# Late modulation and scaled output weights computed by halves of 512 columns, in one or two tiles of h at a time

## The chip, the cores and the metric

The kernel runs on one core of one Trainium2 chip. The metric is the device time of one execution in microseconds, the median of several. Five queues issue instructions in their own order and wait for each other through semaphores: PE (matmuls), DVE (vector), ACT (scalar), POOL (GpSimd) and SP, which here only issues DMA transfers. The program is one straight run without loops on the chip. A list scheduler of the framework fixes the order on each queue when the program is built; the kernel's Python code gives the dependencies and, by the order in which it records work, the priorities.

## The reference

One decoder layer over 2048 tokens of width 1024, in float32. A conditioning vector gives six vectors of 1024 (shift, scale and gate for each of the two sub-layers); two kinds of attention (8 heads each) run side by side; then one output projection, and a gated MLP with a convolution.

```python
mod = jax.nn.silu(c) @ w_ada[l] + b_ada[l]
shift_a, scale_a, gate_a, shift_m, scale_m, gate_m = [
    m[:, None, :] for m in jnp.split(mod, N_MOD, axis=-1)]
h = rms_norm(x, g_attn[l]) * (1.0 + scale_a) + shift_a
proj = h @ w_in[l]
q_f, k_f, v_f, q_s, k_s, v_s, f_logit = jnp.split(proj, offsets, axis=-1)
...
mix = jnp.concatenate([head_rms_norm(o_fox, g_out_fox[l]),
                       head_rms_norm(o_sb, g_out_sb[l])], axis=-1)
x = x + gate_a * (mix @ w_out[l])
h = rms_norm(x, g_mlp[l]) * (1.0 + scale_m) + shift_m
u = causal_depthwise_conv(h @ w_up[l], conv_w[l], conv_b[l])
u_gate, u_val = jnp.split(u, 2, axis=-1)
x = x + gate_m * ((jax.nn.silu(u_gate) * u_val) @ w_down[l])
return rms_norm(x, g_final)
```

The change touches four of the six vectors, those that are needed only after attention: `gate_a` (part 2 of `w_ada`), `shift_m` (3), `scale_m` (4) and `gate_m` (5); and the product of `w_out` with `gate_a` and the heads' gains.

## The kernel before

**Precision.** Each operand of a matmul is split into a high and a low part (`split`, lines 44 to 46: ACT copies and rounds, then DVE or POOL subtracts); a product is three matmuls.

**First half: units of attention.** There are 32 units (line 807): kind `sb` then `fox`, four pairs of heads p each, four blocks tb of 512 tokens each. Unit i's attention (`attend`) is the main stream. Beside it runs `ahead`, the projections of later units. For a unit (kind, p, tb) the projection `proj` (lines 463 to 473) loads the eight split tiles of the normalized input from DRAM, `hp<-hs` (line 468, 512 KB each, named `hs{tb}_{kt}`), and multiplies each at once: L342 for q and k, L413 for v. q, k and v go through DRAM (`qk_fox`, `vs_fox`) and are loaded again per unit as Q, K, V (lines 362 to 364). For each `fox` pair the running sums of the forget gate are loaded as `Fb` (line 653), 4 times 512 KB.

**The tiles of h.** `h_tile()` (line 155) takes one of ten tiles of 128 x 2 x 512 (512 KB) from the pool `sl`, all under one tag. The projections' `hs` loads and the late modulation share these ten; `wide()` (line 158) is the same tile seen as 128 x 1024.

**Late modulation** (`late_mod`, line 756, with `fold_out`, line 743) is a filler. From unit 12 on, `interleave` (line 109) records `PER` of its steps per unit (line 862: `LATE, PER = 12, 3`). For each of four parts it adds up, over eight blocks kt of 128 rows, `w_ada` times the column of `silu(c)`: a load (L776), then ACT scales it (L782) and POOL adds it to `wsum` (L783; L780 for the first). `wsum` holds one tile of h, each load takes another. For the two gates a third tile, `gt`, takes the broadcast `b_ada`; PE sums `wsum` over the partitions with a matmul of ones (L790), DVE adds (L791). For `gate_a`, `fold_out` then loads the eight row blocks of `w_out` (L746, a tile each), multiplies on DVE (L749), splits each half into another tile of h and stores it to `wos` (L753); `gt` stays held for the whole of it. `gate_m` is stored (L796). For shift and scale, eight matmuls of one column (L800) and an add (L802) make the columns `mod_m`.

**Behind it.** At unit 30 the code drains what is left of `ahead` and of `late_mod`, closes the pool `sl` and opens `big` in its place; the output weights are loaded from `wos` (`first_mix`, line 939) and the output projection begins (L912), first beside the last unit's attention. From there to the end the order is mostly fixed by hand (`fixed`, line 206): output projections, then the MLP's matmuls (L1315, L1614).

SP has one queue: a DMA that waits at its head holds back all behind it. Its DMAs also take turns on eight completion semaphores, so a new DMA waits until the one eight places ahead of it has landed.

## Time and profile before

| what | us |
|---|---|
| median of 3 runs | 2948.92 (2948.36 to 2949.31) |
| span of the profiled execution, first to last instruction | 2941.4 |
| its own full time | not on the page; the median less the span is 7.5 |
| PE busy | 2867.8 (97%) |
| DVE, ACT, POOL busy | 2179.5, 1686.0, 901.1 |
| mean granted TensorE clock | 0.993 |

A row of a profile gives engine, line of the kernel, operation, tiles written and read, shape, count and duration. A row of waits says who waited for whom, the sum in us, how often, and the longest. In a timeline a row begins with start and duration, and a bracket at its end gives the idle time before it and what ended it. In a table of windows the columns are the window, its length, busy time of PE, PE's weight loads, DVE, ACT and POOL with their instructions, the granted clock of PE as a share of full speed, the busy share of the DMA engines and the GB/s that they moved.

### The profile page before, as it was taken

Reading aid. Unit: us, or ns where it says so; the run is one execution under the profiler, and the core shown is the slowest. Engines: PE = TensorE matmul, PEld = TensorE weight load, DVE = VectorE, ACT = ScalarE, POOL = GpSimd, SP = SyncE. Lnnn points to the kernel's source line nnn. Section 1 sums busy time; section 2 is a strip of 40 time slices with the busy share of each in tenths; the row PEclk is TensorE's granted clock in tenths of the full one; section 3 lists DMA queues with packets and bytes.
Section 4 is the critical chain, followed back from the end, with each engine's and each line's share of the span. In section 5 each row is a group of like instructions: output and inputs, shape, how many; then the busy total and the mean of one; then the engine's idle time right before and its main releaser. Section 6 shows DMA issues by size and latency. Waiting matters only on the chain.

```text
span 2941.4 us, 45922 instructions
## 1 busy us (share of the span) xinstructions
PE 2867.8 (97%) x15772; PEld 2459.7 (84%) x15772; DVE 2179.5 (74%) x3464; ACT 1686.0 (57%) x3187; POOL 901.1 (31%) x967
## 2 busy tenths in 40 slices
PE   8999999999999999999999999999999999999998
PEld 7888888888988988888888788888788888888887
DVE  5787778877886656658843788888998888575476
ACT  5776767677776656658744554444444445433342
POOL 0431322243032423231213344444254543142200
PEclk8999999999999999999999999999999999999999
DMA  9749756867469794794537775554754444975644
GB/s 293 255 139 321 236 188 207 301 211 229 162 212 356 269 277 139 232 323 140 182 120 233 245 232 128 130 136 129 236 132 125 130 130 132 309 257 185 216 158 151
DMA packets 348346, 601.89 MB, mean 205 GB/s; under 512 B 34672, under 2 KB 178800, under 8 KB 348112
## 3 DMA queue, kind: packets, MB, share of 16 engines
q1 hardware_dynamic: 324208, 558.06, 57.7%
q0 software_dynamic: 10880, 20.97, 4.3%
q10 hardware_dynamic: 13024, 19.93, 1.9%
q8 instruction: 124, 2.03, 0.3%
q14 instruction: 110, 0.90, 0.1%
HBM read 420.77 MB, written 177.02 MB: 203 GB/s over the span
## 4 chain that ended last, share of the span: by engine, by line
PE 46%; DMA 3%; DVE 2%; SPq 1%; ACT 1%; issue 1%; POOL 0%; DVEq 0%; ACTq 0%; POOLq 0%
PE ps_o L1315 19%; PE ps_t L1315 7%; PE ps_o L1614 6%; PE ps_t L1614 3%; PE ps_bc L1614 3%; PE ps_o L912 1%; PE ps_pv L615 1%; DMA r<-rstd 1%; PE ps_bc L912 1%; PE ps_pt L606 1%; PE ps_o L1609 1%; DMA wo<-wos 1%; DMA hm<-hf_m 1%; SPq L895 1%; DVE op L46 1%
## 5 line engine op out<-in xcount | busy, mean ns | idle before, releaser
L1315 PE MATMUL ps_o<-op,wu 128*128 128x512 f32 x2592 | 608.0, 389 | 2.0 <-DVE snap L1366 1.5
L1315 PEld LDWEIGHTS ps_o<-op,wu 128*128 128x128 f32 x2592 | 486.2, 188 | 103.9 <-DVE snap L1366 1.9
L611 DVE TENSOR_TENSOR at<-ps_pt,at 128x512 fp32r<-128x512 f32 (+1 forms) x576 | 366.1, 652 | 100.2 <-ACT at L610 97.3
L636 DVE TENSOR_TENSOR_SCAN a<-r,a 128x512 f32<-128x512 f32 (+2 forms) x320 | 368.3, 1167 | 77.8 <-ACT a L631 39.9
L342 PE MATMUL ps_pj<-hp,w_qk 128*128 128x512 f32 x1512 | 411.2, 403 | 14.5 <-DMA hp<-hs 12.9
L610 ACT ACTIVATE at<-ps_pt 128x512 fp32r<-128x512 f32 (+1 forms) x576 | 318.5, 576 | 139.1 <-PE ps_pt L606 123.1
L615 PE MATMUL ps_pv<-at,V 128*128 128x256 f32 x2216 | 386.8, 292 | 9.3 <-DVE at L611 4.2
L615 PEld LDWEIGHTS ps_pv<-at,V 128*128 128x128 f32 x2216 | 320.9, 190 | 39.8 <-DVE at L611 11.4
L342 PEld LDWEIGHTS ps_pj<-hp,w_qk 128*128 128x128 f32 x1512 | 275.4, 190 | 71.0 <-DMA hp<-hs 16.2
L45 ACT ACTIVATE wu<-wuraw 128x512 fp32r<-128x512 f32 x204 | 128.9, 632 | 248.5 <-PE ps_o L1315 190.1
L596 PE MATMUL ps_qk<-K,Q 128*128 128x512 f32 (+2 forms) x640 | 265.7, 416 | 5.6 <-ACT a L631 3.3
L413 PE MATMUL ps_pj<-w_v,hp 128*128 128x256 f32 (+1 forms) x1536 | 236.6, 288 | 2.1 <-DVE hp L422 1.6
L597 PE MATMUL ps_qk<-K,Q 128*128 128x512 f32 (+2 forms) x640 | 235.7, 369 | 0.0
L1315 PE MATMUL ps_t<-op,wu 128*128 128x512 f32 x888 | 220.8, 390 | 1.0 <-DVE op L46 1.0
L413 PEld LDWEIGHTS ps_pj<-w_v,hp 128*128 128x128 f32 x1536 | 209.0, 189 | 10.9 <-DVE q L373 1.5
L630 ACT ACTIVATE r<-ps_qk 128x512 f32<-128x512 f32 (+2 forms) x320 | 173.1, 541 | 58.2 <-PE ps_qk L597 55.5
L46 DVE TENSOR_TENSOR wu<-wuraw,wu 128x512 fp32r<-128x512 f32 x204 | 189.6, 930 | 18.1 <-ACT wu L45 16.7
L1315 PEld LDWEIGHTS ps_t<-op,wu 128*128 128x128 f32 x888 | 166.4, 188 | 36.5 <-DVE op L46 1.8
L606 PE MATMUL ps_pt<-edge,a 128*128 128x128 f32 x1088 | 185.1, 274 | 8.4 <-DVE a L636 7.8
L1614 PE MATMUL ps_o<-op 128*128 128x512 f32 x840 | 191.5, 389 | 0.0
L1614 PEld LDWEIGHTS ps_o<-op 128*128 128x128 f32 x840 | 157.7, 188 | 32.7
L679 ACT ACTIVATE p<-p,mn 128x128 f32<-128x128 f32 (+15 forms) x128 | 153.9, 1203 | 53.3 <-DVE mn L675 52.2
(342 smaller groups left out, 5237.6 us busy)
## 6 DMA issues: line engine op xcount, KB each, us to landing
hp<-hs SPq DMA_DIRECT2D x224, 512.0 KB
wuraw<-in_w_up_dram SPq DMA_DIRECT2D x80, 512.0 KB
ra<-g SPq DMA_DIRECT2D x136, 256.0 KB
rb<-in_w_down_dram SPq DMA_DIRECT2D x108, 256.0 KB
g<-u SPq DMA_DIRECT2D x80, 256.0 KB
hs<-hp SPq DMA_DIRECT2D x32, 512.0 KB
hp<-in_w_ada_dram SPq DMA_DIRECT2D x32, 512.0 KB
qk_fox<-q SPq DMA_DIRECT2D x32, 512.0 KB
```

What stands on the lines that cost most here:

```text
L46: (lo_engine or nc.gpsimd).tensor_sub(lo, src, f(hi))
L342: nc.tensor.matmul(acc, w[kt][:, a, n], h[:, bb], start=kt == 0 and i == 0, stop=kt == KT - 1 and i == 2)
L413: nc.tensor.matmul(av[:, t * width:(t + 1) * width], hts[kt][:, a, tok], w[1][kt][:, bb, 0:width], start=kt == 0 and m == 0, stop=kt == KT ...
L596: nc.tensor.matmul(b[:, :cw], Q[:, hl, 0, qcols], K[:, hl, :cw], start=True, stop=False)
L597: marks.append(nc.tensor.matmul(b[:, :cw], Q[:, hl, 1, qcols], K[:, hl, :cw], start=False, stop=True).ins)
L606: nc.tensor.transpose(b[:, i * P:(i + 1) * P], blk(kts[kk], qi), ident)
L610: copies = [nc.scalar.activation(at[:, 0, lo:], b[:, lo:], AF.Copy).ins, nc.vector.tensor_sub(at[:, 1, lo:], b[:, lo:], f(at[:, 0, lo:])).ins]
L611: nc.vector.tensor_sub(at[:, 1, lo:], b[:, lo:], f(at[:, 0, lo:])).ins]
L615: m = nc.tensor.matmul(o[:, 0:2 * P], V[kt // 4][:, kt % 4, hl, :], rhs, start=first and kk == 0 and w == 0, stop=last and kk == 1 and w == 1)
L636: nc.vector.tensor_tensor_scan(rev, r[:, 0:need][:, ::-1], rev, 0.0 if right[qi] is None else right[qi][:, 0:1], ALU.mult, ALU.add)
L1315: nc.tensor.matmul(b, w[:, p, j], o[:, q], start=first and i == 0, stop=last and i == 2, skip_group_check=True)
L1614: nc.tensor.matmul(b, a[:, p, t * P:(t + 1) * P], w[:, q], start=first and i == 0, stop=last and i == 2, skip_group_check=True)
```

## The change

All four parts are now computed in two halves of 512 columns. One tile of h per half holds both the sum (`wsum`, its first 512 columns) and the load (`w`, the other 512), so that a load waits until POOL has added the one before it. The broadcast `b_ada` goes into `w`, the gate is made there, and `fold_out` (now called once per half, with the gate in `w`) loads its blocks of `w_out` into the place of `wsum` and takes one other tile of h for each split. The number of `yield`s goes from 56 to 90, and `PER` from 3 to 5.

```diff
-    def fold_out(gt):
+    def fold_out(n, gt, raw):
+        sl = slice(n * TB, (n + 1) * TB)
         for kt in range(KT):
-            raw = wide()
-            nc.sync.dma_start(raw, w_out[kt * P:(kt + 1) * P, :])
-            for n in range(2):
-                sl = slice(n * TB, (n + 1) * TB)
-                nc.vector.scalar_tensor_tensor(raw[:, sl], raw[:, sl], cols[:, R_GF + kt:R_GF + kt + 1], gt[:, sl],
-                                               ALU.mult, ALU.mult)
-                w = h_tile()
-                split(w[:, 0], w[:, 1], raw[:, n * TB:(n + 1) * TB])
-                nc.sync.dma_start(wos[kt][:, :, n * TB:(n + 1) * TB], f(w))
-                yield
+            nc.sync.dma_start(raw, w_out[kt * P:(kt + 1) * P, sl])
+            nc.vector.scalar_tensor_tensor(raw, raw, cols[:, R_GF + kt:R_GF + kt + 1], gt, ALU.mult, ALU.mult)
+            w = h_tile()
+            split(w[:, 0], w[:, 1], raw)
+            nc.sync.dma_start(wos[kt][:, :, sl], f(w))
+            yield
...
         for part, gate in late:
-            wsum = wide()
-            for kt in range(KT):
-                w = wide()
-                nc.sync.dma_start(w, w_ada[kt * P:(kt + 1) * P, part * D:(part + 1) * D])
-                for n in range(0, D, 512):
-                    sl = slice(n, n + 512)
+            for n in range(2):
+                two_ = f(h_tile())
+                wsum, w = two_[:, 0], two_[:, 1]
+                sl = slice(part * D + n * TB, part * D + (n + 1) * TB)
+                for kt in range(KT):
+                    nc.sync.dma_start(w, w_ada[kt * P:(kt + 1) * P, sl])
                     if kt == 0:
-                        nc.gpsimd.tensor_scalar_mul(wsum[:, sl], w[:, sl], cs[:, 0:1])
+                        nc.gpsimd.tensor_scalar_mul(wsum, w, cs[:, 0:1])
                     else:
-                        nc.scalar.activation(w[:, sl], w[:, sl], AF.Copy, scale=cs[:, kt:kt + 1])
-                        nc.gpsimd.tensor_add(wsum[:, sl], wsum[:, sl], w[:, sl])
-                yield
-            if gate is not None:
-                gt = wide()
-                nc.sync.dma_start(gt, b_ada[0:1, part * D:(part + 1) * D].to_broadcast([P, D]))
-                for n in range(2):
+                        nc.scalar.activation(w, w, AF.Copy, scale=cs[:, kt:kt + 1])
+                        nc.gpsimd.tensor_add(wsum, wsum, w)
+                    yield
+                if gate is not None:
+                    nc.sync.dma_start(w, b_ada[0:1, sl].to_broadcast([P, TB]))
                     b = pt()
-                    nc.tensor.matmul(b, ones, wsum[:, n * 512:(n + 1) * 512], start=True, stop=True)
-                    nc.vector.tensor_add(gt[:, n * 512:(n + 1) * 512], b, gt[:, n * 512:(n + 1) * 512])
+                    nc.tensor.matmul(b, ones, wsum, start=True, stop=True)
+                    nc.vector.tensor_add(w, b, w)
                     yield
-                if gate == 0:
-                    yield from fold_out(gt)
+                    if gate == 0:
+                        yield from fold_out(n, w, wsum)
+                    else:
+                        nc.sync.dma_start(gate_m[:, n * TB:(n + 1) * TB], w)
                 else:
-                    nc.sync.dma_start(gate_m, gt)
...
-    LATE, PER = 12, 3
+    LATE, PER = 12, 5
```

For shift and scale each half now makes four matmuls of one column and one add of four columns. Lines of the changed kernel below the edit are 3 lower than before (L912 is L909).

The order on SP moves at three places on which the prediction rests. Names of `hs` tell block and kt (`hs3_7` is the last load of the projection of a unit with tb = 3); `hp` are tiles of h.

**First place**, before: SP at the end of the projection of the unit (fox, pair 2, tb 3), where the K, Q and Fb of the next pair's attention are loaded.

```order
L653 DMA Fb_15443<-fs_243 128x1024
L363 DMA K_15722<-qk_fox2_2_14948 64x512
L362 DMA Q_15461<-qk_fox2_1_14178 64x1024
L653 DMA Fb_15445<-fs_243 128x1024
L362 DMA Q_15461<-qk_fox2_1_14178 64x1024 x3
L363 DMA K_15722<-qk_fox2_2_14948 64x512
L796 DMA gate_m_248<-hp_14928 128x1024
L363 DMA K_15722<-qk_fox2_2_14948 64x512
L468 DMA hp_15772<-hs3_7_91 128x1024
```

The same projection in the changed program, with the semaphores that each row waits for (DMAHW: an earlier DMA's; Pool, PE, DVE: that engine's):

```order
L775 DMA hp_15551<-in_w_ada_dram 128x512 [waits DMAHW6_49,DMAHW5_49,PE_49]
L775 DMA hp_15551<-in_w_ada_dram 128x512 [waits DMAHW7_49,DMAHW6_49,Pool_49]
L775 DMA hp_15551<-in_w_ada_dram 128x512 [waits DMAHW0_49,Pool_49]
L468 DMA hp_15595<-hs3_0_84 128x1024 [waits DMAHW1_49,PE_49]
L468 DMA hp_15600<-hs3_1_85 128x1024 [waits DMAHW2_49,PE_49]
L468 DMA hp_15677<-hs3_2_86 128x1024 [waits DMAHW3_49,PE_49]
L468 DMA hp_15682<-hs3_3_87 128x1024 [waits DMAHW4_49,PE_49]
L775 DMA hp_15551<-in_w_ada_dram 128x512 [waits Pool_49]
L468 DMA hp_15739<-hs3_4_88 128x1024 [waits PE_49]
L468 DMA hp_15744<-hs3_5_89 128x1024 [waits DMAHW7_49,PE_49]
L468 DMA hp_15792<-hs3_6_90 128x1024 [waits DMAHW0_49,PE_49]
L468 DMA hp_15797<-hs3_7_91 128x1024 [waits DMAHW1_49,PE_49]
```

`hs3_7`, which stood behind the burst of Fb, K and Q and behind the store of `gate_m`, now follows `hs3_6` at once, ahead of that burst.

**Second place**, before: SP at the change from fox pair 0 to pair 1, between two loads of the projection (fox, pair 2, tb 1).

```order
L468 DMA hp_14073<-hs1_4_72 128x1024
L363 DMA K_13261<-qk_fox1_1_11941 64x512 x4
L363 DMA K_13512<-qk_fox1_2_12345 64x512
L653 DMA Fb_13242<-fs_243 128x1024
L363 DMA K_13512<-qk_fox1_2_12345 64x512 x3
L653 DMA Fb_13244<-fs_243 128x1024
L362 DMA Q_13260<-qk_fox1_1_11941 64x1024 x4
L440 DMA vs_fox2_0_222<-q2_13722 128x1024
L440 DMA vs_fox3_0_226<-q2_13723 128x1024
L363 DMA K_13989<-qk_fox1_3_12746 64x512 x4
L468 DMA hp_14078<-hs1_5_73 128x1024
```

The same burst in the changed program:

```order
L363 DMA K_13543<-qk_fox1_2_12378 64x512
L653 DMA Fb_13273<-fs_243 128x1024
L363 DMA K_13543<-qk_fox1_2_12378 64x512 x2
L653 DMA Fb_13275<-fs_243 128x1024
L775 DMA hp_12309<-in_w_ada_dram 128x512
L362 DMA Q_13291<-qk_fox1_1_11971 64x1024 x4
L363 DMA K_13543<-qk_fox1_2_12378 64x512
L775 DMA hp_13439<-in_w_ada_dram 128x512
L363 DMA K_14017<-qk_fox1_3_12776 64x512 x4
L783 DMA hp_12309<-in_b_ada_dram 128x512
L363 DMA K_14660<-qk_fox2_0_13236 64x512 x3
L468 DMA hp_14006<-hs1_0_68 128x1024
```

The burst no longer splits the eight `hs1` loads after the fifth; the first of them, `hs1_0`, now stands behind it, with two loads of `w_ada` and one of `b_ada` in it.

**Third place**, after only: the burst of the first place meets another projection, that of (fox, pair 3, tb 2), which now comes earlier.

```order
L468 DMA hp_17360<-hs2_0_76 128x1024
L363 DMA K_15750<-qk_fox2_2_14970 64x512 x2
L653 DMA Fb_15471<-fs_243 128x1024
L363 DMA K_15750<-qk_fox2_2_14970 64x512
L653 DMA Fb_15473<-fs_243 128x1024
L363 DMA K_15750<-qk_fox2_2_14970 64x512
L363 DMA K_16573<-qk_fox2_3_15857 64x512
L362 DMA Q_15489<-qk_fox2_1_14207 64x1024 x4
L363 DMA K_16573<-qk_fox2_3_15857 64x512 x3
L775 DMA hp_16199<-in_w_ada_dram 128x512
L363 DMA K_16973<-qk_fox3_0_16738 64x512 x4
L468 DMA hp_17365<-hs2_1_77 128x1024
```

Here `hs2_1` stands behind a burst of the same kinds, with one load of `w_ada` in it.

More of the change, by code (lines that the diff above doesn't have):

```diff
@@ L792, in late_mod @@
                     yield
-                if gate == 0:
-                    yield from fold_out(gt)
-                else:
-                    nc.sync.dma_start(gate_m, gt)
-            else:
-                cb = pt()
-                for d in range(KT):
-                    nc.tensor.matmul(cb[:, d:d + 1], wsum[:, d * P:(d + 1) * P], ones[:, 0:1], start=True, stop=True)
-                i = 1 if part == 3 else 0
-                nc.vector.tensor_add(mod_m[:, i], cb[:, 0:KT], cols[:, R_BA + part * KT:R_BA + (part + 1) * KT])
-                yield
+                    if gate == 0:
+                        yield from fold_out(n, w, wsum)
+                    else:
+                        nc.sync.dma_start(gate_m[:, n * TB:(n + 1) * TB], w)
+                else:
+                    cb = pt()
+                    for d in range(KT // 2):
+                        nc.tensor.matmul(cb[:, d:d + 1], wsum[:, d * P:(d + 1) * P], ones[:, 0:1], start=True, stop=True)
+                    i = 1 if part == 3 else 0
+                    d0 = n * KT // 2
+                    c0 = R_BA + part * KT + d0
+                    nc.vector.tensor_add(mod_m[:, i, d0:d0 + KT // 2], cb[:, 0:KT // 2], cols[:, c0:c0 + KT // 2])
+                    yield
```

## The prediction

> **What bounds the kernel now.** I begin with the busy times of the page.
>
> ```profile
> span 2941.4 us, 45922 instructions
> PE 2867.8 (97%) x15772; PEld 2459.7 (84%) x15772; DVE 2179.5 (74%) x3464; ACT 1686.0 (57%) x3187; POOL 901.1 (31%) x967
> ```
>
> PE is busy for 97% of the span, and the change adds and removes no large matmul. So it can win only PE's idle time and PE's time at a low clock, and only where the late modulation runs. The table of windows says where that is:
>
> ```profile
> 600.00:1460.00 860.00, 829.31 (x5489) 738.25 (x5489) 619.96 (x1340) 596.82 (x1199) 253.65 (x340) 0.99 0.70 232
> 1660.00:2941.00 1281.00, 1267.70 (x5598) 1047.02 (x5596) 998.98 (x1278) 574.28 (x889) 440.84 (x376) 1.00 0.58 173
> ```
>
> From unit 12 to the last unit PE idles 860 - 829.31 = 30.7 us, at a clock of 0.99. Behind 1660 it is full and its order is fixed by hand; nothing there depends on the fill, and I leave it as it is. Then the waits: for whom does PE idle in this stretch?
>
> ```profile
> PE ps_pj L342 <- DMA hp<-hs: 12.3, 7, 6.0
> PE ps_pt L606 <- DVE a L636: 3.6, 7, 1.1
> PE ps_pv L615 <- DVE at L611: 3.1, 7, 1.0
> PE ps_bc L615 <- ACT at L610: 1.4, 3, 0.6
> ```
>
> The largest item is the projection waiting for its `hs` loads, 12.3 us in 7 waits. The others are short. PE's timeline shows that two of the seven make up most of it:
>
> ```profile
> 1052.80 1.65 PE L342 MATMUL ps_pj<-hp,w_qk 128*128 128x512 f32 x3 [6.01 <-DMA hp<-hs]
> 1208.81 1.65 PE L342 MATMUL ps_pj<-hp,w_qk 128*128 128x512 f32 x3 [3.40 <-DMA hp<-hs]
> ```
>
> Idle PE costs more than its idle time here, as the granted clock of these two stretches of 20 us shows:
>
> ```profile
> 1040.00:1060.00 20.00, 13.99 (x81) 12.28 (x80) 6.99 (x20) 8.97 (x23) 3.25 (x7) 0.83 1.04 295
> 1200.00:1220.00 20.00, 16.60 (x106) 15.34 (x105) 10.85 (x26) 11.48 (x28) 6.31 (x9) 0.83 0.78 253
> ```
>
> A clock of 0.83 over 20 us loses 20 x 0.17 = 3.4 us in each. So **16.2 us** hang on these two waits: 6.0 + 3.4 idle and twice 3.4 of clock.
>
> **Term 1: the first place, a wait that goes.** SP's timeline shows which load came late at 1208.81:
>
> ```profile
> 1198.70 0.33 SPq L796 DMA_DIRECT2D gate_m<-hp  x1
> 1200.74 0.33 SPq L468 DMA_DIRECT2D hp<-hs  x1
> ```
>
> In the order before, the `hs` load right behind the store of `gate_m` is `hs3_7`. It stands there because its tile of h was one of those that the late modulation held. In the new order it follows `hs3_6` ahead of the burst; the modulation holds one or two tiles, so the eight loads find room. Its 3.4 us idle and 3.4 us clock go: **-6.8**.
>
> **Term 2: the second place, the same burst in front of another load.** The wait at 1052.80 ends a burst. These rows give the sizes, and the rate between 1030 and 1056, when the DMA engines were busy throughout:
>
> ```profile
> DMA packets 2627, 7.26 MB, mean 279 GB/s; under 512 B 418, under 2 KB 418, under 8 KB 2626
> ...
> hp<-hs SPq DMA_DIRECT2D x3, 512.0 KB
> K<-qk_fox SPq DMA_DIRECT2D x11, 128.0 KB
> Fb<-fs SPq DMA_DIRECT2D x2, 512.0 KB
> Q<-qk_fox SPq DMA_DIRECT2D x4, 256.0 KB
> vs_fox<-q SPq DMA_DIRECT2D x2, 512.0 KB
> ```
>
> Before, 12 K, 2 Fb, 4 Q, 2 `vs` and `hs1_5` itself are 5120 KB = 5.24 MB, at 279 GB/s 18.8 us. PE waited 6.0 of them, so 12.8 us were covered by other matmuls. In the new order 11 K, 2 Fb, 4 Q, 2 halves of `w_ada`, one of `b_ada` and `hs1_0` are 4736 KB = 4.85 MB, 17.4 us. With the same cover PE waits 17.4 - 12.8 = 4.6 us. A gap of 3.40 cost 3.4 us of clock, so I take 3.4 again. That is 8.0 in place of 9.4: **-1.4**. The bounds are -9.4 (all covered) and, if the cover shrinks by 5 us as in the second rival, +3.6.
>
> **Term 3: the third place, a wait that may come.** The burst freed at the first place now stands ahead of `hs2_1`: 12 K, 2 Fb, 4 Q, one half of `w_ada` and the load are 4352 KB = 4.46 MB, 16.0 us; less 12.8 that is 3.2 us of waiting. What a gap just under 3.4 us does to the clock shows early in the trace, where PE waited for DVE:
>
> ```profile
> 165.94 0.65 PE L564 MATMUL ps_pt<-edge,xt 128*128 128x128 f32 x4 [2.78 <-DVE xm L567]
> ...
> 166.00:168.00 2.00, 1.33 (x9) 1.13 (x10) 1.36 (x2) 1.56 (x5) 1.48 (x2) 0.75 0.46 184
> 168.00:170.00 2.00, 2.00 (x10) 1.70 (x8) 1.94 (x3) 1.35 (x3) 0.77 (x1) 0.50 0.22 85
> ```
>
> After 2.78 us idle the clock fell to 0.50, and these 4 us lost 2 x 0.25 + 2 x 0.50 = 1.5. So 3.2 us of gap lie between 1.5 and 3.4 of clock; I take 3.0, nearer the closer gap: **+6.2**, between 0 and, with 5 us more, +11.6.
>
> [...]
>
> **What is hidden.** The work of the fill itself:
>
> ```profile
> L776 SPq DMA_DIRECT2D hp<-in_w_ada_dram x32: 328/333/2012, 629.7 to 1308.4; - x32
> L782 ACT ACTIVATE hp<-hp,cs x56: 705/714/744, 643.8 to 1320.8; 128x512 f32<-128x512 f32 x56
> L783 POOL TENSOR_TENSOR hp<-hp x56: 1267/1293/2204, 644.6 to 1322.3; 128x512 f32<-128x512 f32 x56
> L749 DVE SCALAR_TENSOR_TENSOR hp<-hp,cols x16: 744/748/1221, 799.1 to 987.8; 128x512 f32<-128x512 f32 x16
> ```
>
> ACT, POOL and DVE run as many of these as before and of the same shape. SP issues 43 more (32 of `w_ada`, 8 of `w_out`, 2 of `b_ada`, 1 of `gate_m`) at 0.333 us, 14.3 us over some 690, while it waits 63.3 us for `oT` alone (below). That is nothing; without this cover each `hs` load behind one is 0.3 us later.
>
> New is the single buffer: a load waits for POOL's add of the step before. Before, a whole load issued at 648.94 was scaled from 652.88 on, right after ACT had waited for it:
>
> ```profile
> 648.94 0.33 SPq L776 DMA_DIRECT2D hp<-in_w_ada_dram  x1
> ...
> 652.88 1.34 ACT L782 ACTIVATE hp<-hp,cs 128x512 f32<-128x512 f32 x2 [0.58 <-DMA hp<-in_w_ada_dram]
> ```
>
> So 3.94 us bound the landing of a half from above; with 0.71 and 1.29 a step takes at most 5.9, and 64 steps 380 us. The 16 of `fold_out` replace the 0.71 by 0.75 on DVE and a split, under 8 us each, 128 in all. Together 508 us, and the fill has from 629.7 to 1322.3, 692 us: it ends in time. If it did not, the output weights would be late, since they wait for its tiles, and with them the filler L912 of the last unit; the stretch ahead of that filler shows what could be lost:
>
> ```profile
> 1323.00:1460.00 137.00, 131.11 (x914) 114.00 (x913) 120.25 (x325) 110.68 (x208) 29.22 (x55) 1.00 0.54 173
> ```
>
> PE fills 131.11 of its 137 us without L912; I put 0.
>
> The waits that the single buffer can lengthen:
>
> ```profile
> ACT hp L782 <- DMA hp<-in_w_ada_dram: 23.5, 17, 4.9
> DVE hp L749 <- DMA hp<-in_w_out_dram: 2.2, 3, 0.9
> SPq L740 <- DVE oT L738: 63.3, 15, 12.4
> SPq L776 <- POOL hp L783: 23.2, 10, 5.0
> SPq L468 <- POOL hp L783: 14.1, 7, 5.0
> ```
>
> ACT waited 23.5 us in 28 loads; 56 loads at the same mean are 47. Queued behind such a wait on ACT are the copies of the transposed attention weights (L610) that DVE and then PE need. PE's wait for them above is 1.4 us, and ACT is busy for 597 of 860 us, so there is room. Bounds: nothing, and 1.4 doubled, +1.4; I take **0**, since none of ACT's 17 waits shows among PE's. DVE's wait doubles to 4.4 us in 860 with 240 idle: 0. The waits of `hs` loads for POOL (14.1) end, but what they delayed was covered except in terms 1 to 3: 0.
>
> **Sum.** Against the profiled execution: 2941.4 - 6.8 - 1.4 + 6.2 = 2939.4. The runs' median is 7.5 above the span, so **2946.9**, 2.0 less.
>
> **The rivals.**
>
> *One or both bursts are covered (faster).* The order puts `hs2_0` ahead of the third burst, and its three matmuls, with attention's, may cover more than 12.8 us. For it: the other five of the seven waits for `hs` were 2.9 us together (12.3 - 9.4), so loads mostly come in time. Against it: the bursts carry nearly the same bytes. Without the third wait the time is 2946.9 - 6.2 = 2940.7; without both, 2948.9 - 16.2 = 2932.7.
>
> *SP waits for POOL with the projection's loads behind it (slower).* At the first place a load of `w_ada` that waits for POOL stands right ahead of `hs3_0`, and in both bursts one stands ahead of the late load. For it: 64 loads now wait this way, and SP's longest wait for POOL was 5.0 us. Against it: 10 such waits brought no visible stall of PE. If POOL is 5.0 late at both bursts, both gaps grow by it: 2946.9 + 10 = 2956.9. It decides from where POOL's add ends later than the matmul that frees the tile of the next `hs` load.
>
> *Halves cost as much as wholes.* Then three halves more in the second place and one in the third add 4 x 0.262 MB at 279 GB/s, 3.8 us: 2950.7. Against it: a burst of pieces of 128 KB kept 279 GB/s. [...]
>
> **How the numbers follow.** My forecast gets 0.40, the covered bursts 0.34, POOL 0.20, dear halves 0.06. The range runs from 2933 (both bursts covered) to 2959 (POOL's case and 2 more for ACT's bound); I leave about 2 in 10 outside, for a schedule that shifts other waits. A change under 0.2%, 5.9 us, cannot be told from none: faster means below 2943.0, slower above 2954.8. Forecast and dear halves lie within: 0.46, of which I move 0.02 to slower, where other waits may add up. Faster 0.34, same 0.44, slower 0.22.
>
> **What would show it.** Term 1: no wait of PE for `hs3_7`. Terms 2 and 3: two gaps of 3 to 5 us on L342 ended by a load of `hs`, one near 1040 us and one, later in PE's order than the wait of before at 1208, near 1240, each in a stretch of 20 us at a clock of about 0.83. If these stretches read 1.00, the first rival holds. The second shows as SP's waits for POOL at the lines of `w_ada` growing from 23.2 us, with an `hs` load next and PE idle for it. I am wrong in kind if PE's idle time between 600 and 1460 changes through DVE or ACT.

## The result, and the profile after

The changed kernel takes **2969.47 us** (median of 6 runs, 2962.18 to 2975.69) against 2949.11 for the kernel before on the same chip: a ratio of 1.0068 (95% interval 1.0052 to 1.0083). It is slower by 20 us, and 10 us above the range that was given. Its profiled execution has a span of 2974.0 us; it is the slowest of the six, so I check below what belongs to the execution and what to the change. The first rows are the page's, then the row of the table of windows that was shown of before:

```profile
span 2974.0 us, 45991 instructions
PE 2883.3 (97%) x15772; PEld 2471.4 (83%) x15772; DVE 2180.0 (73%) x3466; ACT 1686.3 (57%) x3187; POOL 902.5 (30%) x967
```

```profile
600.00:1460.00 860.00, 818.88 (x5376) 728.39 (x5375) 601.79 (x1285) 582.32 (x1175) 243.65 (x326) 0.99 0.71 231
```

DVE and ACT have no more work than before (DVE 2180.0 against 2179.5, ACT 1686.3 against 1686.0). But PE idles 41.1 us in these 860 instead of 30.7. For whom it waits there has changed:

```profile
PE ps_pj L342 <- DMA hp<-hs: 8.7, 7, 2.9
PE ps_pv L615 <- ACT at L610: 7.7, 5, 4.0
PE ps_pv L615 <- DVE at L611: 5.8, 9, 1.8
PE ps_qk L596 <- DVE mn L675: 5.0, 8, 2.4
PE ps_pt L606 <- DVE a L636: 4.3, 8, 0.9
PE ps_pv L615 <- DVE oT L738: 4.1, 4, 2.5
PE ps_pt L606 <- ACT p L679: 3.8, 5, 2.2
```

The wait for `hs`, on which the prediction rested, fell from 12.3 to 8.7 us. In its place PE waits for DVE and ACT. PE's timeline has these gaps of over 1.2 us between 600 and 1500; before there were three:

```profile
710.62 0.96 PE L342 MATMUL ps_pj<-hp,w_qk 128*128 128x512 f32 x3 [1.28 <-DMA hp<-hs]
735.89 0.62 PE L615 MATMUL ps_pv<-at,V 128*128 128x256 f32 x3 [1.83 <-DVE at L611]
910.89 0.44 PE L596 MATMUL ps_qk<-K,Q 128*128 128x384 f32 x1 [2.42 <-DVE mn L675]
971.83 2.29 PE L615 MATMUL ps_pv<-at,V 128*128 128x256 f32 x9 [2.54 <-DVE oT L738]
1065.26 0.93 PE L342 MATMUL ps_pj<-hp,w_qk 128*128 128x512 f32 x3 [2.94 <-DMA hp<-hs]
1146.34 0.39 PE L615 MATMUL ps_pv<-at,V 128*128 128x256 f32 x1 [1.60 <-ACT at L610]
1267.78 0.58 PE L615 MATMUL ps_pv<-at,V 128*128 128x256 f32 x1 [4.04 <-ACT at L610]
1270.27 2.93 PE L342 MATMUL ps_pj<-hp,w_qk 128*128 128x512 f32 x6 [1.90 <-DMA hp<-hs]
1459.23 1.12 PE L606 MATMUL ps_pt<-edge,p 128*128 128x128 f32 x4 [2.25 <-ACT p L679]
```

DVE's timeline names the work behind the gaps at 911 and 972: the product of `fold_out` (L747) at the head of DVE's queue, waiting for its load of `w_out`, with what PE needs queued behind it. ACT's timeline shows the same at 1267, where the scaling of a `w_ada` half waited through a burst of DMA:

```profile
909.41 0.75 DVE L747 SCALAR_TENSOR_TENSOR hp<-hp,cols 128x512 f32<-128x512 f32 x1 [1.69 <-DMA hp<-in_w_out_dram]
...
970.70 0.75 DVE L747 SCALAR_TENSOR_TENSOR hp<-hp,cols 128x512 f32<-128x512 f32 x1 [2.39 <-DMA hp<-in_w_out_dram]
...
1266.53 0.72 ACT L779 ACTIVATE hp<-hp,cs 128x512 f32<-128x512 f32 x1 [6.17 <-DMA hp<-in_w_ada_dram]
```

**What belongs to the execution.** Two rows of SP's timeline for each kernel, of before and then of after, are landmarks: the store of the eleventh unit's output, ahead of which the order is the same in both kernels, and the store of the last unit's output.

```profile
608.04 0.32 SPq L740 DMA_DIRECT2D os<-oT  x1
...
1516.93 1.30 SPq L740 DMA_DIRECT2D os<-oT  x1
```

```profile
619.18 0.32 SPq L740 DMA_DIRECT2D os<-oT  x1
...
1546.00 1.49 SPq L740 DMA_DIRECT2D os<-oT  x1
```

Of the 32.6 us between the two spans, 11.1 arise ahead of the first landmark, 17.9 between the two and 3.5 behind. A second profile of each kernel passes the first landmark at 614.55 (before) and 615.90 (after), so the 11.1 are the execution's. **The change costs about 18 us between the landmarks.** From here on I count PE's loss in 45 windows of 20 us, beginning 12 us behind the first landmark: idle time (length less PE's busy time) plus the time lost to the clock (length times one less the granted clock). It is 36.8 us before and 53.6 after. By stretches, in times of before, with before ahead of after: up to 860, 10.0 and 10.3; from 860 to 1000, **3.4 and 15.6**; to 1100, 9.4 and 6.5; to 1300, 7.9 and 12.1; to 1520, 6.2 and 9.1. The stretch that lost most, 860 to 1000, is where the second half of `fold_out` runs, and no term of the prediction lay there.

### The profile page after: what moved, and what is told of

The parts are those of the page before. It is cut to its first block, busy times and chain, and to the rows that moved or that the text cites. A ratio compares the mean times of both kernels' runs of the same rounds, so it can differ in the third digit from the quotient of the medians.

```text
span 2974.0 us, 45991 instructions
## 1 busy us (share of the span) xinstructions
PE 2883.3 (97%) x15772; PEld 2471.4 (83%) x15772; DVE 2180.0 (73%) x3466; ACT 1686.3 (57%) x3187; POOL 902.5 (30%) x967
## 4 chain that ended last, share of the span: by engine, by line
PE 73%; DMA 12%; DVE 5%; ACT 4%; issue 3%; POOL 2%; SPq 1%; ACTq 0%; DVEq 0%; POOLq 0%
PE ps_o L1312 19%; PE ps_t L1312 7%; PE ps_pj L342 7%; PE ps_o L1611 6%; PE ps_pv L615 6%; PE ps_pt L606 5%; PE ps_pj L413 5%; PE ps_t L1611 3%; PE ps_bc L1611 3%; DMA hp<-in_w_ada_dram 3%; PE ps_qk L596 3%; PE ps_o L909 3%; PE ps_qk L597 2%; DMA hp<-hs 2%; DVE a L636 1%
## 5 line engine op out<-in xcount | busy, mean ns | idle before, releaser
L611 DVE TENSOR_TENSOR at<-ps_pt,at 128x512 fp32r<-128x512 f32 (+1 forms) x576 | 365.8, 651 | 109.9 <-ACT at L610 107.7
L636 DVE TENSOR_TENSOR_SCAN a<-r,a 128x512 f32<-128x512 f32 (+2 forms) x320 | 369.7, 1172 | 80.3 <-ACT a L631 39.7
L342 PE MATMUL ps_pj<-hp,w_qk 128*128 128x512 f32 x1512 | 416.4, 405 | 11.4 <-DMA hp<-hs 8.7
L615 PE MATMUL ps_pv<-at,V 128*128 128x256 f32 x2216 | 394.0, 294 | 20.7 <-ACT at L610 8.3
L610 ACT ACTIVATE at<-ps_pt 128x512 fp32r<-128x512 f32 (+1 forms) x576 | 318.9, 576 | 149.0 <-PE ps_pt L606 129.6
L342 PEld LDWEIGHTS ps_pj<-hp,w_qk 128*128 128x128 f32 x1512 | 275.6, 191 | 66.0 <-DMA hp<-hs 7.4
L596 PE MATMUL ps_qk<-K,Q 128*128 128x512 f32 (+2 forms) x640 | 265.2, 415 | 10.9 <-ACT a L631 5.5
L45 ACT ACTIVATE wu<-wuraw 128x512 fp32r<-128x512 f32 x204 | 129.0, 632 | 252.7 <-PE ps_o L1312 191.3
L413 PEld LDWEIGHTS ps_pj<-w_v,hp 128*128 128x128 f32 x1536 | 210.6, 190 | 10.3 <-DVE q L373 1.3
L46 DVE TENSOR_TENSOR op<-ra,op 128x512 fp32r<-128x512 f32 x144 | 110.1, 770 | 95.9 <-ACT op L45 95.2
```

What stands on the lines that cost most here:

```text
L46: (lo_engine or nc.gpsimd).tensor_sub(lo, src, f(hi))
L342: nc.tensor.matmul(acc, w[kt][:, a, n], h[:, bb], start=kt == 0 and i == 0, stop=kt == KT - 1 and i == 2)
L413: nc.tensor.matmul(av[:, t * width:(t + 1) * width], hts[kt][:, a, tok], w[1][kt][:, bb, 0:width], start=kt == 0 and m == 0, stop=kt == KT ...
L596: nc.tensor.matmul(b[:, :cw], Q[:, hl, 0, qcols], K[:, hl, :cw], start=True, stop=False)
L610: copies = [nc.scalar.activation(at[:, 0, lo:], b[:, lo:], AF.Copy).ins, nc.vector.tensor_sub(at[:, 1, lo:], b[:, lo:], f(at[:, 0, lo:])).ins]
L611: nc.vector.tensor_sub(at[:, 1, lo:], b[:, lo:], f(at[:, 0, lo:])).ins]
```

## The experiments

Each kernel was run beside the kernel before on the same chip; a ratio is to that. They come in the order in which they were made, since each answer changed the question; only the second profile of the changed kernel was taken later, with the first runs of the second question.

### First question: is it the single slot?

Theory A: the one slot for loads makes ACT and DVE stand waiting. Its rivals are the pace and the halves (B), and a loss outside the fill (C).

**Three slots, in halves** (the changed kernel with a second tile):

```diff
-                two_ = f(h_tile())
-                wsum, w = two_[:, 0], two_[:, 1]
+                two_, more = f(h_tile()), f(h_tile())
+                wsum, ws3 = two_[:, 0], (two_[:, 1], more[:, 0], more[:, 1])
...
+                    w = ws3[kt % 3]
...
-                        yield from fold_out(n, w, wsum)
+                        yield from fold_out(n, w, (wsum, more[:, 0], more[:, 1]))
```

> The changed kernel, but each half takes a second tile of h, so that the loads of w_ada rotate over three slots of 512 columns and those of w_out over three: a load runs while the one before it is still used. Order, pace (PER 5) and halves stay. Theory A (the one slot makes ScalarE and VectorE stand at the head of their queues for a load, and the attention's copies behind them come late): ScalarE's wait at L779 falls from 52 us between 600 and 1480 to under 15, PE's waits for ScalarE and VectorE in L615 and L596 return to about the level of before, and the time is 2941 to 2953, 17 to 28 us under the changed kernel. Theory B (the new pace and the halves by themselves disturb the attention): the waits for loads fall, PE's waits do not, and the time stays at 2962 to 2974. Theory C (the loss lies outside the stretch of the late work): the same as B, with PE's waits of 600 to 1480 small in both. The second tile is taken from the attention's hs loads, so the wait at L342 may return to the 12 us of before: up to 6 us of the gain.

Measured: 2965.53 us, 1.0059 (1.0042 to 1.0077). ACT's wait for `w_ada` fell only to 36.1 us, DVE's for `w_out` from 10.3 to 2.4, and the time stayed. DVE's timeline shows why the fall of its wait did not help: the blocks that no longer wait now come together.

```profile
723.31 2.10 DVE L748 SCALAR_TENSOR_TENSOR hp<-hp,cols 128x512 f32<-128x512 f32 x3
725.34 2.45 DVE L636 TENSOR_TENSOR_SCAN a<-r,a 128x512 f32<-128x512 f32 x2
727.71 1.26 DVE L611 TENSOR_TENSOR at<-ps_pt,at 128x512 fp32r<-128x512 f32 x2
```

Three products in a row hold a scan and the copy L611 behind them, and PE has a gap of 2.12 us at 728.42, ended by L611.

**Scaling on GpSimd** (ACT never waits for a load of the fill):

```diff
-                        nc.scalar.activation(w, w, AF.Copy, scale=cs[:, kt:kt + 1])
+                        nc.gpsimd.tensor_scalar_mul(w, w, cs[:, kt:kt + 1])
```

> The changed kernel with the scaling of a w_ada half done on GpSimd instead of ScalarE, so that ScalarE never waits for a load of the late work; the slot stays single, and VectorE still waits for w_out at L747. Theory A: PE's wait for ScalarE at L610 (7.7 us between 600 and 1480) goes back to about 1, the waits for VectorE behind L747 stay, and the time is 2951 to 2961. Theory B: time as the changed kernel, 2962 to 2974. A third way: GpSimd, with twice the work, falls behind, the late work and the hs loads that SyncE issues behind its waits come late, and the time is over 2975.

Measured: 2963.34 us, 1.0051 (1.0033 to 1.0070). PE's wait for L610 fell from 7.7 to 1.4 us as A said, but the waits for DVE did not fall (L636 7.6, L611 6.9), nor did the time: it is above the range of A and in that of B.

**Single slot with whole columns** (the kernel before with one tile for the loads of a part):

```diff
+        raw = wide()
...
-            raw = wide()
...
-            wsum = wide()
+            wsum, w = wide(), wide()
...
-                w = wide()
```

> The kernel before, whole 1024 columns and PER 3, but one tile for all of a part's loads of w_ada and one for all loads of w_out, each reused as soon as it is read: the single slot without the halves and without the new pace. Theory A: ScalarE's wait for w_ada rises from 23.5 us to over 45, VectorE's for w_out from 2 to over 8, and the time is 2958 to 2972. Theory B: 2945 to 2953, as the kernel before.

Measured: 2962.79 us, 1.0048 (1.0033 to 1.0062), and ACT's wait for `w_ada` 47.4 us: as A said; DVE's for `w_out` rose to 5.4 us, less than the 8 of A. With whole columns, where a reload takes twice the bytes, a single slot does cost.

**The kernel before, and the changed kernel, a second time:**

> The kernel before unchanged, for a second profile: how far the stretch before 600 us, whose order the change leaves alone, differs from one execution to the next. Theory C: the store of the fourth pair's output, 608 us in the first profile and 619 in that of the changed kernel, stands anywhere between the two, so that 11 us of the difference between the two profiles belong to the execution and not to the change. If it stands within 2 us of 608, they belong to the change after all.

> The changed kernel once more, for a second profile of it: which of PE's gaps come back at the same place. If the gaps belong to the order of the queues, the gaps of over 1.5 us at about 735, 909, 971, 1065, 1146, 1267, 1270 and 1459 us come back within some 15 us of these times (less what the stretch ahead of 600 us differs), with the same line and engine ahead of them; if they belong to the execution, most stand elsewhere.

Measured: 2945.88 and 2967.88 us, one execution each. The first landmark stood at 614.55 and 615.90, so the 11 us ahead of it are the execution's, as C said; but 18 us remain between the landmarks, and C falls as the cause. PE's loss between the landmarks was 36.0 and 54.1 us (first profiles 36.8 and 53.6). In the second profile of after all nine gaps come back at their places, for the same engine and line, for example:

```profile
908.63 0.69 PE L596 MATMUL ps_qk<-K,Q 128*128 128x384 f32 x1 [2.46 <-DVE mn L675]
970.29 1.33 PE L615 MATMUL ps_pv<-at,V 128*128 128x256 f32 x9 [2.07 <-DVE oT L738]
1062.18 1.62 PE L342 MATMUL ps_pj<-hp,w_qk 128*128 128x512 f32 x3 [3.15 <-DMA hp<-hs]
1263.30 0.58 PE L615 MATMUL ps_pv<-at,V 128*128 128x256 f32 x1 [3.10 <-ACT at L610]
```

Three more of over 1.2 us stand there that the first does not have (2.06 us for `hs` at 877, 1.48 at 928, 1.43 at 1052), and the second profile of before has its three and three others of 1.33 to 1.50. So most of the gaps, and the long ones, belong to the order of the queues.

### Second question: a late load, or the pace?

Theory A2: what hurts is not the number of slots but that a load is issued too shortly ahead of its use.

**Three slots, loads recorded two blocks ahead** (likewise in `fold_out`):

```diff
+                load = lambda k: nc.sync.dma_start(ws3[k % 3], w_ada[k * P:(k + 1) * P, sl]) if k < KT else None
+                load(0), load(1)
                 for kt in range(KT):
-                    nc.sync.dma_start(w, w_ada[kt * P:(kt + 1) * P, sl])
+                    load(kt + 2)
+                    w = ws3[kt % 3]
```

> The changed kernel with three slots of 512 columns as in the first experiment, and each load of w_ada and w_out recorded two blocks ahead of the block that uses it, so that SyncE gets it earlier. Theory A2 (what hurts is not the number of slots but that a load is issued only about 3 us ahead of its use, or 7 us in a burst of DMA, with ScalarE or VectorE standing at its head): ScalarE's wait for w_ada falls under 12 us (52 in the changed kernel, 36 with three slots alone), PE's gaps behind ScalarE and VectorE return to about the level of before, and the time is 2944 to 2955, what is left being the waits for hs. Theory B (halves and pace by themselves): 2960 to 2968 as with three slots alone, though the waits for the loads are gone. If the waits for hs take over (more tiles of h held, the loads earlier in SyncE's queue), L342's wait rises above 18 us.

Measured: 2958.22 us, 1.0039 (1.0021 to 1.0056). PE's wait for ACT at L610 fell to 1.0 us, but L636 (9.1) and L611 (5.5) stayed. ACT's wait was 27.3 us, not under 12. By the ratios some four tenths of the loss went; neither theory has the rest.

**The fill on GpSimd alone** (product and split, and the scaling as above):

```diff
-            nc.vector.scalar_tensor_tensor(raw, raw, cols[:, R_GF + kt:R_GF + kt + 1], gt, ALU.mult, ALU.mult)
+            nc.gpsimd.tensor_scalar_mul(raw, raw, cols[:, R_GF + kt:R_GF + kt + 1])
+            nc.gpsimd.tensor_mul(raw, raw, gt)
...
-            split(w[:, 0], w[:, 1], raw)
+            nc.gpsimd.tensor_copy(w[:, 0], raw)
+            nc.gpsimd.tensor_sub(w[:, 1], raw, f(w[:, 0]))
```

> The changed kernel with the scaling of w_ada, the product of fold_out and its split all on GpSimd, one slot as in the change: neither ScalarE nor VectorE ever waits for a load of the late work. Theory A2: PE's waits of 600 to 1490 for ScalarE and VectorE (about 32 us in the changed kernel) return to the 17 of before, and the time is 2946 to 2957, with hs waits as what is left. Theory B: 2960 to 2970. Third: GpSimd falls behind and SyncE's waits for it hold the hs loads: L342's wait above 18 us, time 2960 and more, but with PE's waits for ScalarE and VectorE as before.

Measured: 3004.49 us, 1.0199 (1.0166 to 1.0232), far above the ranges of A2 and B. The third way had said 2960 and more, with a wait above 18 us at L342 for `hs`, which is 16.9. A new wait of PE, 12.54 us for the split of the next pair's weights (L45), stands at 1066; the run says nothing on A2.

**The kernel before with PER 5:**

```diff
-    LATE, PER = 12, 3
+    LATE, PER = 12, 5
```

> The kernel before with PER 5 in place of 3, nothing else: 56 whole steps recorded within 11 units instead of 18. Theory A2: the loads are as many as before, so ScalarE's wait for w_ada stays under 35 us and the time within 2943 to 2954. Theory B with the pace as its cause: 2958 to 2970.

Measured: 2964.01 us, 1.0057 (1.0040 to 1.0075). **Whole columns, two and three tiles, only the pace changed, and most of the loss is there.** ACT's wait for `w_ada` was 21.4 us, less than before. A2 cannot explain this.

**Halves and single slot at the old pace.** `PER` counts steps, and a step is not the same work in the two kernels: a block of `w_ada` was halved, a block of `fold_out` was not. So PER 5 gives 2.5 whole blocks of `w_ada` per unit instead of 3, but 5 blocks of `fold_out` instead of 3. This kernel restores 3 and 3:

```diff
             nc.sync.dma_start(wos[kt][:, :, sl], f(w))
             yield
+            yield
...
                     nc.vector.tensor_add(w, b, w)
                     yield
+                    yield
...
-    LATE, PER = 12, 5
+    LATE, PER = 12, 6
```

> The changed kernel at the pace of the kernel before: PER 6 over half steps, with a second yield behind each block of fold_out and behind each gate, so that as many columns are recorded per unit as before with PER 3. Single slot and halves stay. If the single slot and the late loads by themselves cost the time (theory A2): 2958 to 2972, with ScalarE's wait for w_ada over 40 us. If the new pace costs it (theory B): 2945 to 2953. If any new order of the queues costs it (theory D: the order of before is a favourable one of many, and each new order has eight or more short gaps of PE in other places): 2955 to 2972, with gaps at other places than in the changed kernel, and not only behind loads.

Measured: **2947.20 us, 1.0000 (0.9984 to 1.0017)**. The whole loss is gone, with halves and the single slot in place, and with ACT waiting for its loads nearly as long as in the changed kernel (52.1 us there):

```profile
ACT hp L780 <- DMA hp<-in_w_ada_dram: 48.1, 30, 3.9
```

So it is neither the slot nor the sum of these waits, and A2 falls as the cause of the whole. What differs is where they stand: the longest is 3.9 us, not 6.2.

**How much does any other order cost (theory D)?** Two small shifts of before, and one of after:

```diff
-    LATE, PER = 12, 3
+    LATE, PER = 12, 3.2
```

> The kernel before with PER 3.2 in place of 3: 7% more pace, same work, same slots, same DMAs. Theory D: another order costs time by itself, 2953 to 2966. Theory A2 or B: nothing here makes a load late or the pace much higher, 2944 to 2952.

```diff
-    LATE, PER = 12, 3
+    LATE, PER = 11, 3
```

> The kernel before with LATE 11 in place of 12: the fill begins one unit earlier, all else as before. Theory D: 2953 to 2966. Theory A2 or B: 2944 to 2952.

```diff
-    LATE, PER = 12, 5
+    LATE, PER = 12, 5.5
```

> The changed kernel with PER 5.5 in place of 5. Theory D: the time moves by several us to either side of the changed kernel's 2969, as another order does, 2955 to 2975. Theory A2: the loads wait as before the edit, 2962 to 2974. Theory B: a higher pace is dearer, 2968 to 2980.

Measured: 1.0016 (1.0006 to 1.0026), 1.0012 (0.9999 to 1.0025), and for after with 5.5 2992.40 us, 1.0139 (1.0115 to 1.0164). The two small shifts of before cost about 5 us at most, so from before D does not reach 20. From the changed kernel it may: a tenth more pace costs 21 us more, above what I expected of any theory, and most of that arises behind 1000 (in times of before), where `fold_out` has ended: PE's loss there is 42.0 us, against 27.8 in the changed kernel. Order is not excluded as a part of the loss.

### Third question: is it the density of fold_out?

Theory F: 5 blocks of `fold_out` per unit instead of 3 are what costs. Theory P: only the place of the steps does.

**The kernel of 1.0000, with 6 blocks of fold_out per unit:**

```diff
             nc.sync.dma_start(wos[kt][:, :, sl], f(w))
             yield
-            yield
```

> The run of halves at the old pace (2947.2), but with one yield behind each block of fold_out instead of two: fold_out at 6 blocks per unit instead of 3, w_ada at 6 halves per unit as there; the parts behind fold_out come about three units earlier. Theory F (fold_out's density is what costs): 2962 to 2990, with new gaps of PE behind VectorE's and ScalarE's work of fold_out between about 700 and 950. Theory P (only the place of the steps, by chance): anything from 2946 to 2975. If 2944 to 2952, F falls.

**The kernel before, with 5 blocks per unit and all else at 3:**

```diff
-                yield
+                if (2 * kt + n) % 5 in (1, 3, 4):
+                    yield
```

> The kernel before, whole columns, PER 3, but fold_out yields after 3 of 5 blocks: 5 blocks per unit as in the change, all else at the old pace. Theory F: 2955 to 2968. Theory P: 2946 to 2960. If under 2951, fold_out's density by itself is not it.

Measured: 2983.54 us, 1.0113 (1.0079 to 1.0146), and 2974.98 us, 1.0093 (1.0066 to 1.0119). One `yield` taken away costs 33 us by the ratios; and with whole columns and the old slots a dense `fold_out` alone costs 28, more than F had said. **Both go F's way**, though both also move the parts behind `fold_out`. PE's waits for DVE in 300 us around `fold_out` show the part of it that lies there. Before (700 to 1000 us):

```profile
PE ps_pt L606 <- DVE a L636: 1.7, 3, 1.1
...
PE ps_pv L615 <- DVE at L611: 1.5, 3, 1.0
...
PE ps_pv L615 <- DVE oT L738: 1.0, 2, 0.8
```

The changed kernel (711 to 1011), and before with 5 blocks per unit (707 to 1007):

```profile
PE ps_qk L596 <- DVE mn L675: 4.2, 6, 2.4
PE ps_pv L615 <- DVE at L611: 4.1, 4, 1.8
PE ps_pv L615 <- DVE oT L738: 3.5, 3, 2.5
```

```profile
PE ps_pt L606 <- DVE a L636: 4.2, 7, 1.5
PE ps_pv L615 <- DVE at L611: 3.0, 3, 1.5
```

The lines are attention's own; DVE comes late to them because the products of `fold_out` stand in its queue ahead of them, alone and waiting (above), or two in a row, as at 924.02 in before with 5 blocks, where 0.85 us of wait and 1.41 us of product stand ahead of L611. (With whole columns the two products of a block come in a row at 3 blocks per unit too, only farther apart.)

That is not the whole loss of that kernel: by the windows 10 of its 28 us lie ahead of 1000. The rest lies at other bursts, where other loads now stand:

```profile
1237.30 1.73 PE L615 MATMUL ps_pv<-at,V 128*128 128x256 f32 x4 [6.86 <-ACT at L610]
1406.45 0.77 PE L596 MATMUL ps_qk<-K,Q 128*128 128x512 f32 x1 [7.11 <-DMA Q<-qk_fox]
```

At 1237 ACT had waited 7.26 us for `w_ada`; at 1406 PE waited for Q of the next unit. A shorter `fold_out` moves all that follows it, so this rest may be the place of the steps, as P says, and not the density itself.

**The old pace with loads recorded two blocks ahead** (the diffs of the loads ahead and of the old pace together):

> The run of halves at the old pace with three slots and each load recorded two blocks ahead. If the waits of ScalarE and VectorE for the late loads cost PE anything at this pace: 2938 to 2945, ScalarE's wait for w_ada from 48 to under 25 us. If they are covered there, as that run says: 2945 to 2953, though the waits fall.

Measured: 2953.42 us, 1.0019 (1.0005 to 1.0033), with ACT's wait at 32.1, less of a fall than expected (under 25), and the time just above the range for covered waits. At this pace taking some of the waits away buys nothing.

**The changed kernel with fold_out later:**

```diff
-        late = ((2, 0), (5, 1), (3, None), (4, None))
+        late = ((5, 1), (2, 0), (3, None), (4, None))
```

> The changed kernel, PER 5, with the parts in the order gate_m, gate_a, shift_m, scale_m, so that fold_out begins about 3.5 units later. If fold_out costs because VectorE is full in the sb units (theory F1): PE's loss from 700 to 1000 falls by 5 us and more against the changed kernel, time 2950 to 2964. If its density costs wherever it stands (theory F2): 2964 to 2985.

Measured: 2967.55 us, 1.0076 (1.0049 to 1.0103): by the time, F2. `fold_out` now runs from 895 to 1132, and PE's waits for DVE go with it (L611 4.4, L675 4.1, `oT` 2.4 between 890 and 1130). But the profiled execution is the shortest of the four (2961.31 us, in F1's range), and in it PE's loss from 700 to 1000 fell from 19.6 to 10.5 us, which was F1's sign; a `fold_out` that has left that stretch gives this under either.

**A thin fold_out, in halves** (PER 8, four yields; the diff is to the kernel with 6 blocks per unit) **and in whole columns** (PER 4.2, two yields; to before):

```diff
             nc.sync.dma_start(wos[kt][:, :, sl], f(w))
             yield
+            yield
+            yield
+            yield
...
-    LATE, PER = 12, 6
+    LATE, PER = 12, 8
```

> Halves with PER 8 and four yields behind each block of fold_out: 2 blocks per unit, w_ada at 8 halves per unit. Theory F: no dearer in the stretch of fold_out than at 3 blocks (8 us lost from 700 to 1000), time 2942 to 2952. If what matters is the place of the later parts against the bursts, which move again: 2950 to 2975, with the loss behind 1000.

```diff
                 nc.sync.dma_start(wos[kt][:, :, n * TB:(n + 1) * TB], f(w))
                 yield
+                yield
...
-    LATE, PER = 12, 3
+    LATE, PER = 12, 4.2
```

> The kernel before, whole columns, PER 4.2 with two yields behind each block of fold_out: 2.1 blocks per unit, w_ada at 4.2 whole blocks. Theory F: 2940 to 2951. If the density of w_ada's loads costs as well, as the run with PER 5 leaves open: 2952 to 2965.

Measured: 2950.31 us, 1.0009 (0.9997 to 1.0021), and 2950.55 us, 1.0010 (0.9996 to 1.0024). Though `w_ada` runs at 4 and 4.2 whole blocks per unit, more than in any kernel above but the one with PER 5 throughout, neither is slow. Nor is one of them faster than before; no version here beats it. One sign of F failed: from 700 to 1000 the thin `fold_out` in halves loses 15.4 us, not 8 (in whole columns 6.1).

All of them side by side, sorted by the density of `fold_out`. "Wait" is PE's for DVE in 300 us from 700 (in times of before), "loss" is idle and clock between the landmarks:

| kernel | blocks of fold_out per unit | ratio | wait, us | loss, us |
|---|---|---|---|---|
| halves, thin fold_out | 2 | 1.0009 | 6.5 | 39.4 |
| whole, thin fold_out | 2.1 | 1.0010 | 3.3 | 38.8 |
| before, two profiles | 3 | 1 | 4.2, 3.5 | 36.8, 36.0 |
| halves, single slot, old pace | 3 | 1.0000 | 3.3 | 36.5 |
| the same, three slots, loads ahead | 3 | 1.0019 | 3.0 | 37.9 |
| before, LATE 11 | 3 | 1.0012 | 4.1 | 43.9 |
| whole, single slot | 3 | 1.0048 | 5.6 | 45.2 |
| before, PER 3.2 | 3.2 | 1.0016 | 6.8 | 40.1 |
| **changed kernel**, two profiles | 5 | 1.0068 | 12.5, 10.8 | 53.6, 54.1 |
| three slots | 5 | 1.0059 | 8.9 | 48.4 |
| scaling on GpSimd | 5 | 1.0051 | 12.8 | 53.7 |
| three slots, loads ahead | 5 | 1.0039 | 8.1 | 49.2 |
| before, PER 5 | 5 | 1.0057 | 7.9 | 47.7 |
| before, dense fold_out | 5 | 1.0093 | 9.6 | 65.2 |
| changed, PER 5.5 | 5.5 | 1.0139 | 10.9 | 64.0 |
| halves, dense fold_out | 6 | 1.0113 | 10.7 | 66.6 |

Left out are the run on GpSimd alone, whose product does not run on DVE, and that with a later `fold_out`, which stands elsewhere (1.0076, loss 45.3). At up to 3.2 blocks PE waits 3.0 to 6.8 us for DVE, at 5 and more 7.9 to 12.8. One row disobeys the ratios: the single slot with whole columns.

The loss has two parts. Ahead of 1000 (in times of before) the kernels of the table with 5 blocks and more lose 22.0 to 34.3 us, those with up to 3.2 lose 11.2 to 20.2. Behind 1000 the groups overlap, at 16.5 to 42.0 and 19.4 to 29.4. The three dearest (before with a dense `fold_out`, PER 5.5 and 6 blocks) lose about 42 there, and in each of them ACT stands 5.8 to 7.3 us at a load of `w_ada`, with a gap of PE of 5.1 to 6.9 us right behind. A gap of about that size occurs in two cheap kernels too (6.95 us with PER 3.2, 4.80 in the thin one with whole columns). So the first part goes with the blocks per unit; the second hangs on where the loads behind `fold_out` then stand, and no run isolated it.

Blocks per unit are what the code records; in time the products lie otherwise. This is DVE's row for the 16 products of the changed kernel; those of before start from 799.1 to 987.8:

```profile
L747 DVE SCALAR_TENSOR_TENSOR hp<-hp,cols x16: 732/750/755, 732.1 to 970.7; 128x512 f32<-128x512 f32 x16
```

In before they stand 12.6 us apart in the mean. In the changed kernel they form two groups of eight, 10.9 us apart up to 808 and 10.1 from 899 on: denser by some 15 to 25%, not by two thirds. In before with 5 blocks they are 8.9 us apart. Nor does the distance alone set the price: the first group of the changed kernel costs nothing (10.3 us of loss up to 860, 10.0 before), and at the old pace with loads ahead the second group stands 7.2 us apart at a ratio of 1.0019.

## Why the prediction was wrong

**The step that failed** is "What is hidden": "ACT, POOL and DVE run as many of these as before and of the same shape", and so the fill's work was priced at nothing. The number of instructions was right, the number per unit was not asked. I had the two figures, 56 to 90 yields and PER 3 to 5, and used them only to ask whether the fill ends in time. That a step of `fold_out` is the same work as before, so that 5 of its blocks are recorded per unit and not 3, appears nowhere. With what it moves, it is worth the 20 us: with the pace of before restored the time is that of before, with 5 blocks alone before loses 28.

**The size that hid it.** "DVE's wait doubles to 4.4 us in 860 with 240 idle: 0" takes the mean over the stretch as room. ACT's wait came out near the 47 that was forecast, DVE's at more than twice its 4.4:

```profile
ACT hp L779 <- DMA hp<-in_w_ada_dram: 52.1, 29, 6.2
DVE hp L747 <- DMA hp<-in_w_out_dram: 10.3, 10, 2.4
```

DVE is not asked for its mean there but for its next copy: a block of 0.75 us of product and up to 2.39 us of wait ahead of it made gaps of 2.4 and 2.5 us. And "none of ACT's 17 waits shows among PE's" was true of before, at the places where those waits then stood; the bound drawn from it, +1.4, was no bound: PE's wait for ACT at L610 grew to 7.7 us.

**Term 1** (-6.8) came: between the gaps at 1146 and 1267 PE has none of over 1.2 us, so `hs3_7` is no longer late. **Term 2** (-1.4) was right in sign and too small: the gap was 2.94 us where I had 4.6, the clock 0.91 over 20 us where I had 0.83, 1.8 instead of 3.4, together -4.7. **Term 3** (+6.2) was in its place and not of its kind: behind the third burst PE idled 4.04 + 1.90 us at a clock of 0.83, 9.3 with the clock. Of the 5.9 idle only 1.90 are the `hs` load. For the rest PE waited for ACT, which stood 6.17 us at a half of `w_ada` in that burst. I had counted this half as bytes ahead of the `hs` load, and not as something at which an engine waits. The three terms together came to -2.2 us, against -2.0 in the sum; that they agree is chance, and the loss lies outside them.

```profile
1060.00:1080.00 20.00, 16.45 (x88) 14.06 (x86) 9.96 (x26) 10.03 (x28) 5.71 (x9) 0.91 0.99 341
...
1260.00:1280.00 20.00, 14.06 (x81) 12.29 (x80) 5.12 (x13) 5.54 (x14) 2.34 (x3) 0.83 0.99 317
```

**The tile itself** was judged rightly in sum: halves and one slot, without the new density, give 1.0000 (0.9984 to 1.0017) where terms 1 to 3 made -2.0 us. But that kernel has another order than the changed one, so it does not confirm the terms one by one.

**The rivals.** SP's wait for POOL at the loads of `w_ada` did grow as the second said:

```profile
SPq L775 <- POOL hp L780: 75.3, 30, 5.2
```

Its price, `hs` loads late behind it, did not come: PE's wait for them fell, from 12.3 to 8.7 us. That its 2956.9 lies nearest to the time is chance. The bursts were not covered, so the first falls. Dear halves fall too: the halves at the old pace are no slower (1.0000). No rival had the density of `fold_out`, while the prediction's last sentence, "I am wrong in kind if PE's idle time between 600 and 1460 changes through DVE or ACT", is what happened.

**What stays open.** Why the single slot costs 14 us with whole columns and nothing with halves at the same pace was not settled. How much of a dense `fold_out` is paid beside it and how much at later bursts differs: 12.5 of 16.8 us lie ahead of 1000 in the changed kernel, 10 of 28 in before with a dense one; the later part goes with places that no run held fixed, so what density costs by itself is known only for the stretch ahead of 1000. One more gap came with the new order: at 1459 the square root of the head norms (L869) stands one block earlier among the exponentials than before, and ACT loads its tables twice with a block of PE's behind it, 2.25 us of PE:

```profile
1454.27 1.28 ACT L869 ACT_TABLE_LOAD   x1
1455.57 0.26 ACT L869 ACTIVATE var<-var 128x64 f32<-128x64 f32 x1
1455.73 0.47 ACT L610 ACTIVATE at<-ps_pt 128x384 fp32r<-128x384 f32 x1
1456.22 1.28 ACT L679 ACT_TABLE_LOAD   x1
```

## What to carry to other kernels

When a filler's steps are cut smaller and its pace in steps is raised to make up for it, work out the new pace for each kind of step: those that were not cut are recorded faster, here 5 blocks of `fold_out` per unit instead of 3. Then look in the trace how much closer they really come, here 15 to 25%. What counted in the second half of `fold_out` was what stood in DVE's queue ahead of the main stream's next instruction, the filler's product and its wait for a load together (0.75 us and up to 2.39, for gaps of 2.4 and 2.5), and DVE's mean busy share of 73% did not show it. ACT's waits for its loads cost nothing in one place (48.1 us in all at the old pace, ratio 1.0000) and several us in another (6.17 us at 1267, with a gap of PE of 4.04 behind it), so before more buffers are bought for such waits, try to thin out the filler.

## What the hardware showed beyond this

The same gap costs the clock in one execution and not in the other. In both profiles of the changed kernel PE idles 1.83 us for L611, at 735.89 and at 732.90. These are the windows of 2 us behind it (the clock is the third number from the right), in the first and in the second:

```profile
736.00:738.00 2.00, 2.00 (x17) 1.92 (x17) 2.00 (x5) 1.10 (x3) 0.56 (x2) 1.00 0.99 367
738.00:740.00 2.00, 1.72 (x9) 1.37 (x9) 2.00 (x5) 0.97 (x2) 0.00 (x0) 1.00 1.02 410
```

```profile
733.00:735.00 2.00, 2.00 (x12) 1.91 (x13) 2.00 (x5) 0.98 (x2) 0.58 (x2) 0.72 0.96 334
735.00:737.00 2.00, 2.00 (x8) 1.80 (x7) 2.00 (x5) 1.09 (x2) 0.00 (x0) 0.50 1.03 418
737.00:739.00 2.00, 2.00 (x9) 1.60 (x9) 1.26 (x2) 0.20 (x1) 0.00 (x0) 0.93 1.06 313
```

The second lost 2 x 0.28 + 2 x 0.50 + 2 x 0.07 = 1.7 us, nearly as much again as the gap; in the first the clock reads 1.00 from 736 to 746. Why one of them lost it and the other did not, no trace here shows. As an estimate from these two gaps alone, one of about 2 us costs between itself and twice itself.
